# Attention in a transformer layer: sums of exponentials made by accumulating transfers

## The chip, the cores and the metric

The kernel runs on one core of a Trainium2 chip. The core has a matrix engine (PE, with PEld for its weight loads), a vector engine (DVE), an activation engine (ACT), a general engine (POOL) and a queue engine (SP); sixteen DMA engines move data. Each engine works through its own instructions in order and waits on semaphores for the others. The metric is device time in microseconds (us): the median of several executions, lower is better. One execution was also profiled; its views are quoted below with the line numbers of the kernel before.

## The reference

One layer works on 2048 latent tokens of width 1024, with 256 context tokens beside them. It normalises and modulates its input, projects it, mixes tokens by two branches (attention and a gated MLP over chunks), merges them, and ends in a wide MLP. The change touches attention alone, of which the reference says:

```python
def attend(q, k, v):
    s = jnp.einsum('bkgqd,bknd->bkgqn', q, k, preferred_element_type=jnp.float32)
    p = jax.nn.softmax(s, axis=-1).astype(v.dtype)
    return jnp.einsum('bkgqn,bknd->bkgqd', p, v)
...
        k_all = jnp.concatenate([k_c, k_x], axis=2)
        v_all = jnp.concatenate([v_c, v_x], axis=2)
        attn_x = merge_heads(attend_blocked(q_x, k_all, v_all))
```

There are 8 query heads of width 64 on 2 key heads, and 256 + 2048 = 2304 keys. The denominator of the softmax is, for every query and head, the sum of 2304 exponentials. Everything is float32.

## The kernel before

The stages follow one another: projections, attention (about 739 to 1341 us of the profiled span), the merge of the branches, the MLP.

**Units.** Attention is cut into 16 units (class `Unit`), for 4 blocks of 512 queries and 4 pairs of heads, numbered 0 to 15 here. A unit goes over 18 tiles of 128 keys in 9 cycles of two tiles (`PAIR`, `CYCLES`, method `attend`). For a tile, `scores` makes the scores of both heads on PE (line 2488, into a tile s of PSUM), and ACT writes their exponentials (line 2494) to an SBUF tile of 128 partitions (keys) by 2 x 512 columns (heads, queries), 512 KB. The even tile of a cycle is a buffer with the tag p2, the odd one with the tag t4; there are eight of each. The profile leaves numbers out, so they are called p and t there. One cycle later `values` multiplies the exponentials with the values on PE (line 2502, into o), and `gather` adds them into an accumulator.

**Sums.** There are two accumulators a unit. Five of the 18 tiles (2, 5, 8, 11, 14; `ON_VECTOR`) go into one that DVE adds (line 2519); the other thirteen into one that POOL adds, half a tile at a time (line 2522). The first tile of each is taken as it stands, so POOL makes twelve adds of two halves and DVE four. The sums have the tag ac, four buffers. In cycles 2 and 4 of the next unit `join` adds DVE's accumulator into POOL's on DVE, a head at a time (line 2537), and in cycle 5 `sums` multiplies the result with ones on PE (line 2544), which adds over the keys. ACT copies that out (line 2550), and it goes to memory.

**Other work of the stage.** The exponentials are taken against a maximum that must be known before a unit begins. So in every cycle PE also makes plain scores for a later unit (line 2431, into banks m of PSUM, three of them, which line 2544 and others share), and DVE takes their maxima (lines 2436, 2441, into ts). Line 2466 spreads a maximum by eight small transfers a unit. DVE also carries a part of another matrix product (line 428) and, in the last three units, prepares inputs of the merge (lines 1536 and 1543). The last unit has no later unit to make maxima for, and its own division of tiles (`LAST_ON_VECTOR`).

**What sets the order.** Each method issues in the order of the source. A scheduling layer assigns buffers and semaphores; for PE and DVE the order of the attention stage is held as written, for ACT and POOL the scheduler chooses it. A tile's buffer is free once all that read it are done.

Of the kernel before, what the change touches and what calls it, by code (L numbers as in the profile page):

```python
# [14 lines left out]
ALU = mybir.AluOpType  # L15
# [54 lines left out]
PAIR = 2  # L70
CYCLES = NKT // PAIR
AHEAD = 6
ON_VECTOR = (2, 5, 8, 11, 14)
LAST_ON_VECTOR = (2, 4, 7, 8, 9, 12, 13, 14, 15)

OPENING = """
# [24 lines left out]
class Kern:  # L101
# [1308 lines left out]
    def attend(self, units, late, mod, key_loads):  # L1410
        self.psum({"s": 2, "m": 3, "o": 1})
        self.nc.gpsimd.memset(self.rg["q"], 0.0)
        begin = self.here()
        n = len(units)
        pend = []

        def ordered(work):
            at = self.here()
            work()
            self.loads.append(range(at, self.here()))  # L1420

        for i, u in enumerate(units):
            at = lambda k: units[k] if 0 <= k < n else None
            nxt, far, old, older = at(i + 1), at(i + 2), at(i - 1), at(i - 2)
            u.banks()
            for c in range(CYCLES):
                step = nxt if c < AHEAD else far
                if c == 0 and far:
                    far.load()
                if step:  # L1430
                    step.maxima(1)
                group = range(PAIR * c, PAIR * (c + 1))
                for j in group:
                    u.scores(j)
                if step:
                    step.maxima(1)
                owner = u if c else old
                for j in pend:
                    owner.values(j)
                if c == 0:  # L1440
                    if old:
                        old.leave()
                    u.o = self.bank([TB], tag="o")
                if c == 5 and old:
                    old.sums()
                if c == AHEAD and nxt:
                    nxt.reference()
                    ordered(nxt.leading)
                for j in pend:
                    owner.gather(j)  # L1450
                if i and c in (1, 7):
                    next(mod, None)
                if c == 1 and older:
                    older.inverse()
                if c in (2, 4) and old:
                    old.join(c // 4)
                if i == 0:
                    next(key_loads, None)
                if i + c / CYCLES > n - 4 and c % 3 == 1:
                    ordered(lambda: next(late, None))  # L1460
                pend = list(group)
        for _ in mod:
            pass
        owner = units[-1]
        for j in pend:
            owner.values(j)
            owner.gather(j)
        units[-2].inverse()
        total = [self.sb("raw", [TB]) for _ in range(2)]
        for h in range(2):  # L1470
            units[-1].join(h, total)
        self.fixed.append(range(begin, self.here()))
# [924 lines left out]
class Unit:  # L2397
# [109 lines left out]
    def gather(self, j):  # L2507
        k, nc = self.k, self.nc
        pt = self.pts.pop(j)
        e = j in (LAST_ON_VECTOR if self.last else ON_VECTOR)  # L2510
        old = self.acc.get(e)
        if old is None:
            self.acc[e] = pt
            return
        if e not in self.own:
            self.own.add(e)
            self.acc[e] = k.sb("ac", [2, TB])
        if e:
            nc.vector.tensor_tensor(out=self.acc[e], in0=old, in1=pt, op=ALU.add)
        else:  # L2520
            for h in range(2):
                nc.gpsimd.tensor_tensor(  # L2522
                    out=self.acc[e][:, h], in0=old[:, h], in1=pt[:, h], op=ALU.add
                )
# [6 lines left out]
        self.nc.scalar.dma_start(k.at_d[self.b][self.p * P : (self.p + 1) * P, :], oc)  # L2531

    def join(self, h, out=None):
        a, v = self.acc[False], self.acc[True]
        if out is None:
            out = [a[:, i] for i in range(2)]
        self.nc.vector.tensor_tensor(out=out[h], in0=a[:, h], in1=v[:, h], op=ALU.add)
        self.total = out

# [77 lines left out]
```

## Time and profile before

| What | Value |
|---|---|
| Median of 3 runs | 2978.05 us (2977.15 to 2979.62) |
| Profiled execution: time | 2976.75 us |
| Profiled execution: span | 2975.0 us |
| Mean granted clock of PE over the span | 0.993 |
| Busy share: PE, PEld, DVE, ACT, POOL | 97%, 74%, 69%, 47%, 21% |
| POOL's adds of line 2522, 774 to 1345 us | 356 half tiles |
| Instructions | 39180 |

Busy shares are means over stages that differ: POOL works almost only in attention. PE's busy time is modelled from pipelined matmuls, so a busy PE may hide short waits; the length of a unit from the first score matmul to that of the next is firmer. In rows of groups and waits, an arrow names what an engine waited for. In rows of the timeline the first two numbers are start and length in us, and the brackets hold the idle time before.

### The profile page before, as it was taken

How to read it: one execution, taken by the hardware profiler on the slowest of the kernel's cores; microseconds unless marked ns; L12 is line 12 of the kernel's file. 1: busy time of each engine (PE TensorE's matmuls, PEld its weight loads, DVE VectorE, ACT ScalarE, POOL GpSimd, SP SyncE). 2: the span in 40 equal slices, each digit the busy share in tenths (PEclk: the TensorE clock that was granted, in tenths of full speed). 3: DMA queues.
4: the chain of work that ended last, by engine and by line, in shares of the span. 5: the costliest groups of instructions: out<-in, count | busy, mean ns of one | idle time of the engine just before them, and what ended most of it. 6: DMA issues, size and time to landing. Idle time of an engine off the chain costs nothing. (4 is left out here: it accounts for less than half of the span.)

```text
span 2975.0 us, 39180 instructions
## 1 busy us (share of the span) xinstructions
PE 2896.6 (97%) x14126; PEld 2190.4 (74%) x14126; DVE 2056.0 (69%) x3018; ACT 1391.5 (47%) x1993; POOL 633.5 (21%) x444
## 2 busy tenths in 40 slices
PE   8989999989999999999999999999999999999999
PEld 7878788767554554447888878887888888878887
DVE  6866486856888888876555688775766766654555
ACT  6545865552554554553222354444453444444442
POOL 0000000000999999982221100000000000000000
PEclk9999999999999999999999999999999999999999
DMA  8688866876110100117776578888766444457654
GB/s 309 193 296 289 308 203 225 266 243 205 59 37 26 36 30 30 40 47 235 215 211 199 156 249 310 305 288 306 260 217 229 169 140 151 152 174 261 217 213 151
DMA packets 392947, 569.09 MB, mean 191 GB/s; under 512 B 39264, under 2 KB 194576, under 8 KB 392752
## 3 DMA queue, kind: packets, MB, share of 16 engines
q1 hardware_dynamic: 380448, 545.87, 54.6%
q10 hardware_dynamic: 12304, 20.71, 1.9%
q8 instruction: 111, 1.82, 0.3%
q14 instruction: 84, 0.69, 0.1%
HBM read 383.82 MB, written 182.58 MB: 190 GB/s over the span
## 5 line engine op out<-in xcount | busy, mean ns | idle before, releaser
L2441 DVE TENSOR_REDUCE ts<-m 128x1 f32<-128x512 f32 x472 | 300.3, 682 | 55.5 <-PE m L2431 53.4
L2045 DVE TENSOR_TENSOR b<-b,b 128x1024 fp32r<-128x1024 f32 x170 | 200.8, 1222 | 136.1 <-ACT b L2044 135.3
L2522 POOL TENSOR_TENSOR ac<-ac,p 128x512 f32<-128x512 f32 x160 | 266.9, 1691 | 39.5 <-ACT p L2494 39.3
L2044 ACT CAST b<-b 128x1024 fp32r<-128x1024 f32 x170 | 170.6, 1050 | 223.4 <-PE b L1929 100.1
L1928 PE MATMUL b<-b,b 128*128 128x512 f32 x680 | 265.6, 391 | 2.9 <-DVE b L2045 2.9
L1927 PE MATMUL b<-b,b 128*128 128x512 f32 x680 | 266.4, 392 | 1.6 <-DVE f L2066 1.4
L1929 PE MATMUL b<-b,b 128*128 128x512 f32 x680 | 265.1, 390 | 0.0
L2494 ACT ACTIVATE p<-s 128x1024 f32<-128x1024 f32 x149 | 152.2, 1025 | 221.6 <-PE s L2488 203.2
L2522 POOL TENSOR_TENSOR ac<-ac,t 128x512 f32<-128x512 f32 x184 | 251.2, 1393 | 6.3 <-ACT t L2494 6.3
L2488 PE MATMUL s<-h,h 64*128 64x512 f32 x1728 | 227.9, 392 | 0.0
L2488 PEld LDWEIGHTS s<-h,h 64*128 64x128 f32 x1728 | 161.6, 185 | 39.6 <-ACT t L2494 4.1
L1928 PE MATMUL b<-hb,b 128*128 128x512 f32 x446 | 174.3, 391 | 0.0
L1937 DVE TENSOR_TENSOR f<-f,b 128x512 f32<-128x512 f32 x160 | 109.3, 683 | 83.1 <-issue 48.9
L1929 PE MATMUL b<-hb,b 128*128 128x512 f32 x415 | 161.9, 391 | 0.0
L1927 PE MATMUL b<-hb,b 128*128 128x512 f32 x415 | 161.9, 390 | 0.0
L2502 PE MATMUL o<-p,h 128*64 128x512 f32 x596 | 160.1, 619 | 0.0
L1928 PEld LDWEIGHTS b<-b,b 128*128 128x128 f32 x680 | 127.7, 188 | 31.6 <-DVE b L2045 5.0
L1927 PEld LDWEIGHTS b<-b,b 128*128 128x128 f32 x680 | 127.7, 188 | 29.6 <-ACT b L2044 2.3
L1929 PEld LDWEIGHTS b<-b,b 128*128 128x128 f32 x680 | 127.7, 188 | 26.3
L2431 PEld LDWEIGHTS m<-h,h 64*128 64x128 f32 x584 | 60.1, 184 | 117.7 <-DVE ts L2441 94.9
L2502 PE MATMUL o<-t,h 128*64 128x512 f32 x556 | 143.8, 596 | 0.0
L2494 ACT ACTIVATE t<-s 128x1024 f32<-128x1024 f32 x139 | 141.5, 1018 | 0.0
(468 smaller groups left out, 7060.3 us busy)
## 6 DMA issues: line engine op xcount, KB each, us to landing
ao_d<-f SPq DMA_DIRECT2D x224, 256.0 KB
f<-in_w_ff SPq DMA_DIRECT2D x48, 1024.0 KB
b<-ao_d SPq DMA_DIRECT2D x85, 512.0 KB
b<-w2o_d SPq DMA_DIRECT2D x85, 512.0 KB
w2o_d<-f SPq DMA_DIRECT2D x112, 256.0 KB
f<-in_w_in SPq DMA_DIRECT2D x38, 512.0 KB
f<-x_d SPq DMA_DIRECT2D x64, 256.0 KB
hb<-ao_d SPq DMA_DIRECT2D x54, 256.0 KB
```

Source lines behind the costliest of these rows:

```text
L1927: mm(ps, wh, hh, start=start and k == 0, stop=False, skip_group_check=True)
L1928: mm(ps, wh, hl, start=False, stop=False, skip_group_check=True)
L1929: mm(ps, wl, hh, start=False, stop=k == len(w) - 1, skip_group_check=True)
L1937: nc.vector.tensor_tensor(out=out, in0=in0, in1=in1, op=op)
L2044: nc.scalar.copy(h, f32(l))
L2045: nc.vector.tensor_tensor(out=l, in0=f32(l), in1=f32(h), op=ALU.subtract)
L2431: nc.tensor.matmul(out, self.q[0][rows, tok], key[rows], start=True, stop=True)
L2441: nc.vector.tensor_reduce(out=self.mx[:, t, h, c : c + 1], in_=ps[h], axis=AX.X, op=ALU.max)
L2488: nc.tensor.matmul(s[:, h], w[rows], x[rows], start=j < PAIR and n == 0, stop=n == len(terms) - 1, skip_group_check=True,)
L2494: nc.scalar.activation(pt, s, AF.Exp)
L2502: nc.tensor.matmul(self.o[h * HD : (h + 1) * HD, :], k.V[c][:, i, self.kv * HD : (self.kv + 1) * HD], pt[:, h], start=j == 0, stop=j == NK ...
L2522: nc.gpsimd.tensor_tensor(out=self.acc[e][:, h], in0=old[:, h], in1=pt[:, h], op=ALU.add)
```

## The change

Every unit but the last gets three accumulators, and tile j goes to number j modulo 3. Number 0 stays with POOL's adds: tiles 0, 3, 6, 9, 12 and 15, five adds of two halves. Numbers 1 and 2 begin as the exponential tiles 1 and 2 themselves; the tiles that follow (five for each) are added by a transfer that POOL issues, from the tile into the accumulator, with the addition done on the way. `join` becomes two such transfers, of numbers 1 and 2 into number 0, both heads at once. `sums` moves from cycle 5 to cycle 7 of the next unit. The last unit works as before.

```diff
-ON_VECTOR = (2, 5, 8, 11, 14)
+SUMMED = 3
...
-                if c == 5 and old:
+                if c == 7 and old:
                     old.sums()
...
         pt = self.pts.pop(j)
-        e = j in (LAST_ON_VECTOR if self.last else ON_VECTOR)
+        e = j in LAST_ON_VECTOR if self.last else j % SUMMED
         old = self.acc.get(e)
         if old is None:
             self.acc[e] = pt
+            return
+        if e and not self.last:
+            nc.gpsimd.dma_start(out=old, in_=pt, accum_op=ALU.add)
             return
         if e not in self.own:
             self.own.add(e)
...
     def join(self, h, out=None):
-        a, v = self.acc[False], self.acc[True]
+        a, v = self.acc[0], self.acc[1 if self.last else 1 + h]
         if out is None:
-            out = [a[:, i] for i in range(2)]
+            self.nc.gpsimd.dma_start(out=a, in_=v, accum_op=ALU.add)
+            self.total = [a[:, i] for i in range(2)]
+            return
```

The first place is POOL, from the end of unit 1 into unit 2; ac is an accumulator of POOL's, t and p are exponential tiles, and x2 stands for the two halves. Before:

```order
L2522 TENSOR_TENSOR ac_7701<-ac_7701,t_1443_7932 128x512 x2
L2522 TENSOR_TENSOR ac_7701<-ac_7701,p_1448_7962 128x512 x2
L2522 TENSOR_TENSOR ac_7701<-ac_7701,t_1449_7970 128x512 x2
L2522 TENSOR_TENSOR ac_8068<-p_1459_8006,t_1460_8016 128x512 x2
L2522 TENSOR_TENSOR ac_8068<-ac_8068,t_1468_8056 128x512 x2
L2522 TENSOR_TENSOR ac_8068<-ac_8068,p_1476_8088 128x512 x2
```

After the change:

```order
L2525 TENSOR_TENSOR ac_7730<-ac_7730,t_1439_7910 128x512 x2
L2516 DMA t_1389_7642<-p_1446_7946 128x1024
L2516 DMA p_1396_7672<-t_1447_7954 128x1024
L2539 DMA ac_7730<-t_1389_7642 128x1024
L2539 DMA ac_7730<-p_1396_7672 128x1024
L2525 TENSOR_TENSOR ac_8087<-p_1457_7990,t_1466_8038 128x512 x2
L2516 DMA t_1458_8000<-p_1473_8067 128x1024
L2516 DMA p_1465_8030<-t_1474_8075 128x1024
L2525 TENSOR_TENSOR ac_8087<-ac_8087,p_1480_8103 128x512 x2
L2516 DMA t_1458_8000<-t_1481_8111 128x1024
L2516 DMA p_1465_8030<-p_1486_8137 128x1024
```

The adds now alternate with two transfers each, and both joins (line 2539) stand ahead of the next unit's first add.

The second place is DVE in unit 14, around the preparing operations of lines 1536 and 1543; ts takes the maxima of banks m. Before:

```order
L2519 TENSOR_TENSOR ac_12548<-p_2301_12446,t_2313_12499 128x1024
L2441 TENSOR_REDUCE ts_12008<-m_12550 128x1
L2441 TENSOR_REDUCE ts_12008<-m_12551 128x1
L2441 TENSOR_REDUCE ts_12008<-m_12572 128x1
L2441 TENSOR_REDUCE ts_12008<-m_12573 128x1
L2537 TENSOR_TENSOR ac_12085<-ac_12085,ac_12166 128x512
L1536 TENSOR_TENSOR in_12208<-raw_12346,in_12470 128x512
L1543 TENSOR_TENSOR raw_12590<-in_12474,gx_12476 128x512
L2441 TENSOR_REDUCE ts_12008<-m_12597 128x1
L2441 TENSOR_REDUCE ts_12008<-m_12598 128x1
```

After the change:

```order
L2441 TENSOR_REDUCE ts_11893<-m_12420 128x1
L2441 TENSOR_REDUCE ts_11893<-m_12421 128x1
L2441 TENSOR_REDUCE ts_11893<-m_12442 128x1
L2441 TENSOR_REDUCE ts_11893<-m_12443 128x1
L1536 TENSOR_TENSOR in_12086<-raw_12222,in_12341 128x512
L1543 TENSOR_TENSOR raw_12459<-in_12345,gx_12347 128x512
L2441 TENSOR_REDUCE ts_11893<-m_12466 128x1
L2441 TENSOR_REDUCE ts_11893<-m_12467 128x1
```

The add and the join are gone, and the preparing operations stand directly behind the maxima.

## The prediction

> **What bounds the kernel now.** I read the page's engine row first, then the attention stage cut at the first score matmul of each unit of work (windows; columns: length, then busy time and instructions of PE, PEld, DVE, ACT, POOL, granted clock, DMA share, GB/s).
>
> ```profile
> PE 2896.6 (97%) x14126; PEld 2190.4 (74%) x14126; DVE 2056.0 (69%) x3018; ACT 1391.5 (47%) x1993; POOL 633.5 (21%) x444
> ...
> 848.81:885.75 36.94, 36.94 (x233) 18.77 (x230) 32.28 (x46) 18.89 (x21) 35.72 (x25) 1.00 0.11 37
> 885.75:922.73 36.98, 36.98 (x234) 18.79 (x231) 32.33 (x46) 18.89 (x21) 35.75 (x25) 1.00 0.11 36
> 922.73:961.89 39.16, 38.44 (x234) 19.06 (x232) 32.96 (x47) 18.89 (x21) 36.94 (x27) 1.00 0.12 39
> 1110.34:1149.83 39.49, 38.78 (x235) 19.23 (x232) 33.13 (x46) 18.89 (x21) 36.88 (x27) 1.00 0.09 32
> 1186.77:1223.71 36.94, 36.94 (x232) 18.61 (x230) 30.88 (x44) 19.80 (x23) 34.88 (x25) 1.00 0.14 47
> 1223.71:1264.33 40.62, 38.05 (x234) 18.96 (x230) 36.99 (x49) 20.53 (x24) 36.84 (x25) 1.00 0.14 46
> 1264.33:1306.52 42.19, 37.72 (x214) 17.50 (x210) 34.78 (x39) 20.43 (x24) 33.74 (x23) 0.96 0.08 27
> ```
>
> A middle unit takes 36.94 us and PE works through all of it; that is its floor, since the change leaves PE's instructions as they are. POOL is busy 35.7 of the 36.9 but bounds nothing: it lags and catches up. So taking adds from DVE and POOL earns nothing in the middle units. Only where PE waits can time be won, and PE's waits in the whole stage (774 to 1345 us) are these:
>
> ```profile
> PE m L2431 <- DVE ts L2441: 8.5, 6, 3.0
> PE s L2488 <- DMA h<-t: 0.2, 1, 0.2
> ```
>
> PE waits for DVE to empty a bank of m, 8.5 us in six places. Two, 0.7 us each, are in units 5 and 10 (923 and 1110 us: PE is busy that much less than the length); the other four, 7.0 us, fall into units 13 and 14 (1223 to 1306 us), where DVE also prepares the next stage (lines 1536, 1543). DVE ahead of the longest, and then PE's four:
>
> ```profile
> 1285.43 1.67 DVE L2537 TENSOR_TENSOR ac<-ac,ac 128x512 f32<-128x512 f32 x1
> 1287.02 1.77 DVE L1536 TENSOR_TENSOR in<-raw,in 128x512 fp32r<-128x512 f32 x1
> 1288.72 1.74 DVE L1543 TENSOR_TENSOR raw<-in,gx 128x512 f32<-128x512 f32 x1
> 1290.38 1.87 DVE L2441 TENSOR_REDUCE ts<-m 128x1 f32<-128x512 f32 x3
> ...
> 1247.13 0.50 PE L2431 MATMUL m<-h,h 64*128 64x512 f32 x1 [1.34 <-DVE ts L2441]
> ...
> 1261.69 0.50 PE L2431 MATMUL m<-h,h 64*128 64x512 f32 x1 [1.23 <-DVE ts L2441]
> ...
> 1275.86 0.50 PE L2431 MATMUL m<-h,h 64*128 64x512 f32 x1 [1.47 <-DVE ts L2441]
> ...
> 1291.12 0.49 PE L2431 MATMUL m<-h,h 64*128 64x512 f32 x1 [3.00 <-DVE ts L2441]
> ```
>
> A join, then two preparing operations, 5.2 us in a row, stand ahead of the maximum that PE needs at 1291.12. The clock then falls:
>
> ```profile
> 1291.92:1295.33 3.41, 3.41 (x10) 0.97 (x8) 3.41 (x5) 1.03 (x2) 3.15 (x2) 0.50 0.00 0
> ```
>
> **What the change removes.** From DVE: all adds into its accumulator and both joins of every unit but the last. In units 13 and 14 these are
>
> ```profile
> L2519 DVE TENSOR_TENSOR ac<-ac,p 128x1024 f32<-128x1024 f32 x5 | 8.1, 1628 | 3.8 <-ACT p L2494 3.8
> L1536 DVE TENSOR_TENSOR in<-in,in 128x512 fp32r<-128x512 f32 x4 | 6.1, 1517 | 0.0
> L1543 DVE TENSOR_TENSOR raw<-in,gx 128x512 f32<-128x512 f32 x4 | 6.0, 1491 | 0.0
> L2537 DVE TENSOR_TENSOR ac<-ac,ac 128x512 f32<-128x512 f32 x4 | 5.3, 1320 | 0.0
> ...
> L2519 DVE TENSOR_TENSOR ac<-ac,t 128x1024 f32<-128x1024 f32 x2 | 3.5, 1759 | 0.0
> L2519 DVE TENSOR_TENSOR ac<-p,t 128x1024 f32<-128x1024 f32 x2 | 2.8, 1407 | 0.0
> ```
>
> 8.1 + 5.3 + 3.5 + 2.8 = 19.7 us of DVE's 36.99 + 34.78 = 71.8. POOL's adds fall from twelve tiles a unit to five. That shortens DVE's remaining work too, for the two engines hold each other up. A preparing operation takes 1.7 to 1.8 us beside a POOL add and this when POOL is idle:
>
> ```profile
> 1296.66 0.68 DVE L1536 TENSOR_TENSOR in<-raw,in 128x512 fp32r<-128x512 f32 x1
> 1297.26 0.68 DVE L1543 TENSOR_TENSOR raw<-in,gx 128x512 f32<-128x512 f32 x1
> ```
>
> POOL adds will fill about 12.6 of 37 us instead of 35.7, so a third of such operations meet one: 0.68 + 1.1/3, about 1.05 us each. For the 3.00 us wait: less 1.67 for the join and 2 x 0.7 for the shorter pair leaves nothing. The wait of 1.47 has no join ahead but gains the same 1.4; those of 1.34 and 1.23 lose a join or an add of 1.3 to 1.6 us (the means above), and 0.7 or more. I leave 0.5 of the 7.0 us, and 0.7 of the 1.5 us in units 5 and 10: **won 7.3 us** (bounds: 3.0, if only joins directly ahead go, 1.34 + 1.67, to 8.5). The clock at 0.50 for 3.41 us costs half of it, 1.7 us; without the gap before it I count it **won 1.7** (bounds 0 and 1.7). Unit 13 is 40.62 - 36.94 = 3.7 us long over its floor, of which 2.6 are PE's waits; the rest is small slips: **won 0.5** (0 to 1.1). Sum 9.5 us, bounds 3.0 to 11.3.
>
> The Trainium skill ("TensorE: Matmul & The Clock Gate", Part 1) halves the clock after an idle window of about 3.4 us. Here it fell after 3.0, so the trace is stricter. By the page's figure the drop would not hang on this wait and might stay: the time would be 1.7 us higher.
>
> **What it adds.** Per unit twelve accumulating transfers of 512 KB from POOL's queue, ten sums and two joins, in the order shown above: (add, sum into accumulator 1, sum into accumulator 2) five times, join, join. A sum waits on POOL for the previous transfer into its accumulator; the first join for the last sum of accumulator 1, the second for the first. Behind the waiting one stand all of POOL's later adds and sums; ACT waits for those, as an exponential needs a free tile of t4 or p2 (eight each), and PE waits for the exponentials. So the question is whether POOL gets through a unit in 36.94 us. The add, alone on POOL (minimum/median/maximum ns):
>
> ```profile
> L2522 POOL TENSOR_TENSOR ac<-ac,t x172: 1258/1277/2279, 781.9 to 1319.9; 128x512 f32<-128x512 f32 x172
> ```
>
> Two halves, 2.52 us. The trace of before has no transfer from POOL's queue and none that accumulates. The nearest of the same size and row length (4 KB) goes to memory from SP's queue, issued here, with the DMA share of 0.1 us slices from 1428.2 on:
>
> ```profile
> 1428.25 0.33 SPq L1614 DMA_DIRECT2D x_d<-xt  x1
> DMA  0000000059999999899998922896999999974001
> ```
>
> Data run from slice 8 (1429.0) for thirteen slices: 0.75 us after the issue, 1.3 us long. What follows the data shows in a lone 256 KB transfer, issued at 816.61, in slices of 87.5 ns from 816.5:
>
> ```profile
> 816.61 0.35 ACTq L2531 DMA_DIRECT2D at_d<-t  x1
> DMA  0000000000079999996900000000002000000000
> ```
>
> Data end in slice 19, the closing write comes in slice 30, 0.95 us later. An accumulating transfer reads two tiles: its data time is between 1.3 us (second read free) and 2.6 (twice); I take 2.6, because two tiles must be read. The time that an issue holds POOL lies between the 0.33 above and the longest one of the stage:
>
> ```profile
> L2466 SPq DMA_DIRECT2D h<-t x104: 502/587/1652, 803.8 to 1259.2; - x104
> ```
>
> 1.65. I take 1.0, the middle. Landing after the start of the issue: issue + 0.42 + data + 0.95, so 3.0, 5.0 and 5.6 us for low, taken and high. A round is the greater of POOL's work (2.52 + two issues: 3.2, 4.5, 5.8) and two transfers on the engines (2.6, 5.2, 5.2). POOL's unit is four rounds, the last add, two landings (last sum, first join) and an issue:
>
> - low: 4 x 3.2 + 2.52 + 6.0 + 0.3 = 21.6 us
> - taken: 4 x 5.2 + 2.52 + 10.0 + 1.0 = 34.3 us
> - high: 4 x 5.8 + 2.52 + 11.2 + 1.65 = 38.6 us
>
> Two of three are under 36.94, and there the transfers cost PE nothing: PE's own work covers them. They add 12 x 2.6 = 31 us of transfer time a unit to a DMA share of about 0.11, so the engines are nearly full but hold. Without cover each microsecond over is paid in up to 14 units. At 34.3 the joins have landed some 15 us into the next unit; the sums' matmul now stands in its eighth of nine cycles of about 3.9 us, at about 29 us, and doesn't wait. In its old place, the sixth cycle, 21 us, it would have had 6 us less.
>
> The Trainium skill ("Collectives: The Full Stack", Part 3) states that a reducing transfer takes twice a copy's time because it reads two sources. With one read the middle case would be 4 x 4.5 + 2.52 + 7.4 + 1.0 = 28.9 us, also under the floor; no run here shows it yet.
>
> The last unit keeps its adds and joins on POOL and DVE, and the stages behind it are unchanged; they start earlier by what is won.
>
> **Rivals.**
>
> 1. *POOL's queue becomes the bound* (slower). The mechanism is the chain of issues and landings above; it decides once POOL's unit passes 36.94, with doubled data from an issue of about 1.5 us. At 1.65 it is 38.6, 1.7 us over, in some 8 to 14 units after the free tiles are used up: +13 to +23, less the gain: 2982 to 2992. At 2.0 (landing 6.0, round 6.5) it is 26.1 + 2.52 + 12 + 2.0 = 42.6, 5.7 over in about 12 units: +68 - 9 = 3037. With an issue as long as POOL's own add of such a tile, 2.52, it is 48.3, and about 3105. For it: no row shows an issue from POOL, each row has two sources where a copy has one, and at the taken values only 2.6 us are left. Against: half of the bounded range is under the floor, and POOL may lag by several cycles.
> 2. *Too little is won to see.* Lines 1536 and 1543 stay as long as they are (POOL's issues hold DVE as its adds did) and only what joins and adds held up comes back, 3 to 5 us: 2973 to 2975. For it: the pair alone makes the 1.47 us wait. Against: the 0.68 us rows.
> 3. *The sums wait for the joins.* If landings come near 8 us, the joins need some 24 us and in the units after a late start pass 29: PE would stand there 2 to 4 us a unit, 14 times, 2997 to 3025. Against: eight is beyond the high bound.
>
> **How the numbers follow.** The profiled execution took 2976.75 us, its span 2975.0; the median of the runs is 2978.05, 1.3 more. The span falls to 2965.5, the run to 2967.3, and against the median 2978.05 - 9.5 = **2968.5 us**. A change of under 0.2%, 6 us, can't be told from none here. Chances: forecast 0.57, rival 1 0.28, rival 2 0.12, rival 3 0.03. The forecast's own range is 2965 to 2973. With a low end of 2964 about 3 in 100 lie below; of rival 1 the smaller half ends near 3010, so the range is 2964 to 3010 with some 15 in 100 above. Of the forecast's 0.57 some 0.02 win less than 6 us, and rival 2 adds 0.02 above it and 0.10 below. Rival 1 may come out level with its smallest excess (0.01). Faster 0.57, same 0.13, slower 0.30.
>
> **What would show it.** Right: units 13 and 14 near 37 to 38 us, PE's waits on the maxima under 2 us, granted clock 1.00 around 1290 us, POOL's issues near 1 us and no wait of ACT for transfers. Wrong: units of the middle longer than 37 us, ACT waiting for a transfer into t or p, PE after it; or issues of POOL over 1.5 us. If the waits in units 13 and 14 stay with DVE at 1.7 us for the pair, rival 2 it was.

## The result, and the profile after

The changed kernel is slower: a median of 3018.4 us (3017.23 to 3023.74, four runs) against 2978.84 us of the kernel before (2977.15 to 2980.31, four runs), a ratio of 1.0141 with a 95% interval of 1.0129 to 1.0153. The prediction was 2968.5 us, with a range of 2964 to 3010. Times here and below leave out one execution of the run late_dve, which took 3970.53 us at a granted clock of 0.674.

The page of the changed kernel: the busy rows, and the new DMA queue with its packets, MB and share of the sixteen engines over the whole span.

```profile
PE 2904.8 (96%) x14126; PEld 2192.5 (73%) x14126; DVE 1958.2 (65%) x2928; ACT 1392.4 (46%) x1993; POOL 446.9 (15%) x414
...
q0 software_dynamic: 25920, 94.38, 16.7%
```

DVE lost 98 us of work and POOL 187, as the change says, and nothing was won. The windows from unit to unit show where the time went (columns as in the prediction: length, busy time of PE, PEld, DVE, ACT, POOL, granted clock, DMA share, GB/s).

```profile
771.03:814.12 43.09, 38.77 (x233) 19.93 (x230) 24.34 (x39) 18.99 (x21) 26.07 (x25) 0.96 0.94 185
814.12:852.29 38.17, 37.41 (x233) 18.52 (x230) 25.89 (x40) 18.04 (x21) 20.38 (x20) 1.00 0.91 186
929.47:974.72 45.25, 41.52 (x235) 20.76 (x232) 25.13 (x40) 19.34 (x22) 26.88 (x27) 0.92 0.94 184
1209.30:1251.86 42.56, 39.30 (x233) 19.36 (x230) 23.31 (x37) 19.80 (x23) 23.68 (x24) 0.96 0.94 195
1294.04:1344.30 50.26, 42.02 (x212) 19.51 (x213) 30.36 (x30) 20.49 (x25) 28.37 (x28) 0.86 0.94 193
```

From the first unit's start to the last one's it was 567.9 us before and is 608.2 now: the whole loss of 40 us lies there. Over units 1 to 14 the DMA share stands at 0.89 to 0.94 where it was about 0.1. PE's waits from 774 to 1380 us:

```profile
PE s L2488 <- DMA h<-t: 22.5, 13, 4.3
PE m L2431 <- DVE ts L2441: 11.9, 6, 5.7
PE s L2488 <- ACT p L2494: 3.5, 4, 1.7
```

Of these 0.2, 8.5 and nothing were there before. The first row is new. The transfers h<-t are the eight small ones that spread a unit's maximum (line 2466, 0.5 KB each, from SP's queue). Every unit's first score matmuls need them, and in 13 units they wait. SP's queue where it was longest, and PE behind it:

```profile
920.86 8.65 SPq L2466 DMA_DIRECT2D h<-t  x8
...
933.59 0.76 PE L2488 MATMUL s<-h,ones 64*128 64x512 f32 x1 [3.73 <-DMA h<-t]
```

SP's issuing of the eight took 6.5 to 8.65 us here and 4.9 to 6.0 before. The one shown ended as the unit began, at 929.5, and PE waited until 933.6. After three of the longer waits for the row, of 4.32, 3.73 and 2.26 us, the granted clock fell to 0.50 for 3.4 to 6.8 us; after one of 3.13 us, at 1132, it did not. These falls (0.04 of 43 us, 0.08 of 45, 0.04 of 43) cost 7.0 us; 0.14 of 50 us in unit 14, another 7.0, came behind waits for ACT and DVE. Together that is 14 us, against 1.7 before. So 22.3 for the row, 12 for the clock, 3.4 for DVE and 3.5 for ACT make 41 us, about the loss. DVE is no faster beside POOL either, in unit 14:

```profile
1319.56 4.05 DVE L1536 TENSOR_TENSOR in<-raw,in 128x512 fp32r<-128x512 f32 x1
1323.53 3.72 DVE L1543 TENSOR_TENSOR raw<-in,gx 128x512 f32<-128x512 f32 x1
...
1327.91 0.79 PE L2431 MATMUL m<-h,h 64*128 64x512 f32 x1 [5.66 <-DVE ts L2441]
```

The pair of preparing operations takes 7.8 us where it took 3.5, although POOL has far fewer adds.

### The profile page after: what moved, and what is told of

The parts are those of the page before. It is cut to its first block, busy times and chain, and to the rows that moved or that the text cites. A ratio compares the mean times of both kernels' runs of the same rounds, so it can differ in the third digit from the quotient of the medians.

```text
span 3015.4 us, 39121 instructions
## 1 busy us (share of the span) xinstructions
PE 2904.8 (96%) x14126; PEld 2192.5 (73%) x14126; DVE 1958.2 (65%) x2928; ACT 1392.4 (46%) x1993; POOL 446.9 (15%) x414
## 5 line engine op out<-in xcount | busy, mean ns | idle before, releaser
L2488 PE MATMUL s<-h,h 64*128 64x512 f32 x1728 | 238.4, 399 | 1.0 <-ACT p L2494 1.0
L2488 PEld LDWEIGHTS s<-h,h 64*128 64x128 f32 x1728 | 169.3, 188 | 40.4 <-ACT p L2494 3.9
L1927 PEld LDWEIGHTS b<-b,b 128*128 128x128 f32 x680 | 127.7, 188 | 29.5 <-ACT b L2044 2.3
L2431 PE MATMUL m<-h,h 64*128 64x512 f32 (+1 forms) x584 | 125.9, 420 | 12.5 <-DVE ts L2441 12.5
L1940 ACT ACTIVATE f<-f 128x512 f32<-128x512 f32 x96 | 60.5, 630 | 145.5 <-DVE f L1937 145.5
```

The costliest lines, as they stand in the source:

```text
L1927: mm(ps, wh, hh, start=start and k == 0, stop=False, skip_group_check=True)
L1940: nc.scalar.activation(out, src, AF.Relu)
L2431: nc.tensor.matmul(out, self.q[0][rows, tok], key[rows], start=True, stop=True)
L2488: nc.tensor.matmul(s[:, h], w[rows], x[rows], start=j < PAIR and n == 0, stop=n == len(terms) - 1, skip_group_check=True,)
```

## The experiments

Each was timed beside the kernel before on the same chip. The times of before differ a little from chip to chip, so the ratios count.

| Run | Time, us | Ratio to before, 95% interval |
|---|---|---|
| top_early | 3018.75 | 1.0146 (1.0126 to 1.0167) |
| plain_copies | 2960.18 | 0.9948 (0.9932 to 0.9964) |
| half | 3004.01 | 1.0095 (1.0077 to 1.0114) |
| late_dve | 3014.24 | 1.0127 (1.0105 to 1.0149) |
| joins_only | 3029.09 | 1.0187 (1.0170 to 1.0204) |
| joins_pause | 2993.65 | 1.0063 (1.0046 to 1.0080) |
| pool_joins | 3000.36 | 1.0089 (1.0071 to 1.0107) |
| mix | 2982.78 | 1.0028 (1.0016 to 1.0040) |
| mix_early | 2980.01 | 1.0014 (1.0005 to 1.0023) |
| issue_only | 2983.20 | 1.0025 (1.0015 to 1.0034) |
| ten | 2978.19 | 1.0006 (0.9997 to 1.0015) |
| eleven | 2992.97 | 1.0054 (1.0041 to 1.0066) |
| twelve | 3000.12 | 1.0084 (1.0072 to 1.0097) |
| ten_tail | 2984.81 | 1.0029 (1.0018 to 1.0040) |
| ten_tail2 | 2972.88 | 0.9994 (0.9978 to 1.0009) |
| nine_tail | 2966.48 | 0.9968 (0.9959 to 0.9978) |

### Is it the late row?

**top_early**: the changed kernel with the next unit's maximum finished and sent one cycle earlier. The edit adds two lines, so later lines stand two higher.

```diff
-AHEAD = 6
+AHEAD = 5
...
+                if i == 0 and c == 4:
+                    nxt.maxima(2)
```

> Row theory (the eight small transfers of the next unit's maximum row, line 2466, come late through full DMA engines, and PE waits for them and loses its clock): issued one cycle, 3.9 us, earlier they are in time in nearly all units. The waits of line 2488 for h<-t fall from 22.5 us to under 4, the clock loss of 13.7 us by at least 6, and the time from 3018 to 2983-2993 us. Queue theory (POOL's chain of adds and transfers is the bound and the row's wait only stands where another one would come): another wait takes its place, the unit stays near 40 us and the time at or above 3008.

The row's wait went entirely, and the time stayed. Windows of four units:

```profile
777.19:813.96 36.77, 36.77 (x233) 18.43 (x230) 24.36 (x39) 18.90 (x21) 19.95 (x20) 1.00 0.90 180
...
850.75:887.54 36.79, 36.79 (x232) 18.38 (x230) 24.71 (x39) 18.90 (x21) 20.02 (x20) 1.00 0.91 190
...
1049.14:1090.55 41.41, 38.69 (x232) 18.61 (x230) 25.24 (x39) 18.95 (x22) 23.12 (x22) 0.96 0.91 185
1090.55:1130.89 40.34, 37.33 (x233) 18.29 (x230) 26.16 (x40) 19.01 (x22) 23.09 (x22) 1.00 0.92 181
```

ACT's waits of that run, 774 to 1380 us:

```profile
ACT p L2496 <- DMA ac<-p: 50.3, 12, 5.7
ACT t L2496 <- DMA ac<-t: 26.9, 8, 5.0
```

Units 1 to 3 run at the floor, 36.8 us. From unit 4 on they take 39 to 44: ACT now waits for tiles that a join (ac<-p, ac<-t) frees late. So the row theory holds for the first units only, and behind the row lies a second limit at nearly the same height: POOL's transfers run late a little more in each unit, until no free tile is left. POOL issues a unit's first join 7.7 us into the next unit at first, then 13.1, 18.2 and 22.3, and from there on 23 to 27. In the changed kernel the late row slowed PE before that showed: there ACT waited for no sum and no join. POOL's unit is read from its issues into accumulator 2 in the first and the last round of a unit, its two joins, and the first round of the next unit, from unit 8 into unit 9 of the same run:

```profile
1083.89 1.54 POOL L2518 DMA_DIRECT2D p<-t  x1
...
1111.41 0.88 POOL L2518 DMA_DIRECT2D p<-t  x1 [0.92 <-DMA p<-p]
1114.82 0.87 POOL L2541 DMA_DIRECT2D ac<-t  x1 [2.53 <-DMA t<-p]
1120.53 0.86 POOL L2541 DMA_DIRECT2D ac<-p  x1 [4.85 <-DMA ac<-t]
...
1124.14 1.53 POOL L2518 DMA_DIRECT2D p<-t  x1
```

Four rounds take 27.5 us, 6.9 each; then 3.4 to the first join, 5.7 to the second and 3.6 into the next unit: 40.25 us.

### Is it the length of a transfer?

**plain_copies**: the sums copy, they do not add.

```diff
-            nc.gpsimd.dma_start(out=old, in_=pt, accum_op=ALU.add)
+            nc.gpsimd.dma_start(out=old, in_=pt)
...
-        nc.scalar.copy(row, sm)
+        nc.scalar.activation(row, sm, AF.Copy, bias=1.0)
```

> The ten sums of a unit are plain copies of the tile into the accumulator (the additions of twelve tiles out of eighteen are left out, and 1.0 is added to the denominator so that it stays above zero); the two joins still add. The order on every engine, POOL's issues and all waits stay. Row theory by way of full engines: a plain packet of 4 KB takes about half the time, the DMA share falls from 0.91 to about 0.5 and the row's wait from 22.5 us to under 5: 2983-2995 us. If POOL's issues or the mere number of transfers delay the row, the wait stays above 12 us and the time above 3005.

It is 0.5% faster than before, and far below both outcomes of the expectation: not only the row's wait goes. The queue from 774 to 1380 us, first of the changed kernel, then of this one; then its landings and one of its units:

```profile
q0 software_dynamic: 24800, 90.25, 79.6%
...
DMA to landing us min/median/max: 4.6/5.7/8.9
```

```profile
q0 software_dynamic: 24685, 89.85, 44.4%
...
DMA to landing us min/median/max: 2.8/3.4/7.6
...
845.72:882.47 36.75, 36.75 (x233) 18.35 (x230) 25.67 (x39) 18.91 (x21) 19.95 (x23) 1.00 0.62 206
```

Of 606 us, 0.796 spread over 172 transfers (90.25 MB) are 2.8 us of all sixteen engines for an accumulating transfer; for these it is 1.6. A sixth of these are joins, which still add; at 2.8 for each of them the plain ones are left with about 1.3, an estimate. With the engines 0.62 full, the same order of work on every engine runs at the floor, with no wait for the row and none for DVE's maxima. POOL's issues became shorter too (median 0.53 to 0.57 us against 0.87 to 1.2), so this run alone leaves open how much of it is the engines and how much POOL. It does show that the gain that was predicted was there to be had.

**half**: accumulator 2 goes back to DVE's adds, seven transfers a unit.

```diff
-        if e and not self.last:
+        if e == 1 and not self.last:
```

> Only accumulator 1 is summed by transfers, accumulator 2 by DVE as before (line 2519 form), joins by transfers: 7 transfers a unit, not 12. Row theory: the DMA share falls to about 0.55 and the row is rarely late, its wait under 5 us; DVE has its adds back (5 a unit), so its waits in units 13 and 14 stay near 8 to 12 us: 2978-2990 us. Queue theory: POOL's chain has 5 issues less, the same fall; this run tells the size of the cost per transfer, not the two theories apart. If the loss goes with the number of transfers evenly, the time is 2979 + 39 x 7/12 = 3002.

With the accumulating transfers at 0.46 of the engines the row waited 0.2 us, as expected, but the time was 3004, far over the 2978 to 2990 of the expectation, and close to what an even price per transfer gives, for another reason. PE waited 26.8 us for DVE, in 14 places, and DVE's first add of a unit was long:

```profile
L2522 DVE TENSOR_TENSOR ac<-p,t 128x1024 f32<-128x1024 f32 x14 | 54.3, 3875 | 0.0
L2522 DVE TENSOR_TENSOR ac<-ac,t 128x1024 f32<-128x1024 f32 x29 | 36.5, 1259 | 5.4 <-ACT t L2494 5.4
```

3.9 us against 1.26: DVE is held up beside POOL, which is the next question. For the row, this run answers what plain_copies left open: POOL's issues had their full length here (0.88 us in the median), and the row was not late. So it is neither their number nor their length; what the late row goes with is how full the engines are. From 774 us to the last unit's start the DMA share was 0.58 here, 0.61 in plain_copies and 0.92 in the changed kernel, and the row waited 0.2, 0 and 22.5 us; in pool_joins and mix below, with the row in the same place, it waited 13.0 us at 0.80 and 7.8 at 0.68.

### What holds DVE up?

**late_dve**: in units 12 to 14 DVE makes POOL's adds.

```diff
-        if e:
+        if e or (self.b * (NH // 2) + self.p) >= 12:
             nc.vector.tensor_tensor(out=self.acc[e], in0=old, in1=pt, op=ALU.add)
```

> The changed kernel, but in units 12 to 14 DVE makes the sums of accumulator 0 (whole tiles) and POOL only issues transfers. If POOL's pairs of adds hold DVE's preparing operations (lines 1536, 1543): those of units 13 and 14 fall from up to 4.05 us to about 0.7, PE's waits for DVE from 11.9 us to under 5, and with the clock the time falls by 6 to 12 us, to 3006-3012. If POOL's issuing of transfers holds DVE: they stay above 1.5 us, and the time stays at 3014-3022.

Lines 1536 and 1543 fell to 0.67 and 0.69 us and PE's waits for DVE from 11.9 to 2.1 us. So POOL's adds hold DVE, and its issues alone do not. The time did not fall as expected: at 3014.2 us the ratio cannot be told from the changed kernel's 1.0141, for the row (23.7 us) and ACT (9.6) took the room.

**joins_only**: the kernel before with one transfer a unit.

```diff
-                if c in (2, 4) and old:
-                    old.join(c // 4)
+                if c == 2 and old:
+                    old.join(0)
...
-            out = [a[:, i] for i in range(2)]
+            self.nc.gpsimd.dma_start(out=a, in_=v, accum_op=ALU.add)
+            self.total = [a[:, i] for i in range(2)]
+            return
```

The sums move to cycle 7 as in the change.

> The kernel before with one accumulating transfer a unit: the join of DVE's accumulator into POOL's, both heads at once; all sums stay on POOL and DVE as before, and the sums' matmul is two cycles later. If POOL's issuing of transfers changes nothing for DVE: DVE's adds stay at 1.4-1.5 us (whole tiles), DVE loses its joins (1.3 us each), PE's waits for DVE in units 13 and 14 fall from 8.5 to 3-5 us: 2970-2976. If a DVE operation with two SBUF inputs, in a program whose POOL issues transfers, waits until POOL's run of adds ends: DVE's adds rise above 3 us in the mean, PE waits for DVE in most units, and the time is above 2990.

This is the slowest of all, with a DMA queue that is 7% busy. It is the second outcome, though not in every part: DVE's adds of whole tiles took 1.4 to 2.2 us in the mean, not above 3; what grew most is line 428. Its POOL, DVE and PE around one issue:

```profile
1108.00 0.88 POOL L2536 DMA_DIRECT2D ac<-ac  x1 [0.41 <-POOL ac L2522]
1108.61 2.82 POOL L2522 TENSOR_TENSOR ac<-p,t 128x512 f32<-128x512 f32 x2
1111.09 2.82 POOL L2522 TENSOR_TENSOR ac<-ac,t 128x512 f32<-128x512 f32 x2
1113.73 2.60 POOL L2522 TENSOR_TENSOR ac<-ac,p 128x512 f32<-128x512 f32 x2
1124.86 3.51 POOL L2522 TENSOR_TENSOR ac<-ac,p 128x512 f32<-128x512 f32 x2 [8.53 <-ACT p L2494]
...
1110.70 6.18 DVE L428 SCALAR_TENSOR_TENSOR raw<-raw,silu,raw 128x512 f32<-128x512 f32 x1
...
1125.81 1.41 DVE L2519 TENSOR_TENSOR ac<-p,t 128x1024 f32<-128x1024 f32 x1
...
1118.35 0.79 PE L2431 MATMUL m<-h,h 64*128 64x512 f32 x1 [4.97 <-DVE ts L2441]
```

The operation of line 428, alone 0.74 us, lasts until POOL's three adds behind the issue end at 1116.3, and half a microsecond more. After POOL has rested (8.53 us) its adds let DVE in as before: 1.41 us for a whole tile at 1125.81. Over the run, line 428 took 4.95 us in the mean in the six places where POOL ran on from an issue, and 1.83 in the eight where it did not.

**joins_pause**: one more POOL instruction, which makes POOL rest until the transfer has landed.

```diff
             self.nc.gpsimd.dma_start(out=a, in_=v, accum_op=ALU.add)
+            self.nc.gpsimd.tensor_copy(out=v[:, 0, :1], in_=a[:, 0, :1])
```

> The kernel of joins_only (3029 us) with one more POOL instruction behind the transfer of a unit: a copy of one column of the joined accumulator, which waits until the transfer has landed (about 5 us in which POOL rests). Hold theory (POOL's adds directly behind an issue shut out DVE's two-input operations until POOL next rests; joins_only showed L428 at 4.95 us in the mean there and 1.83 elsewhere): the rest ends the hold, L428 falls to 1.9 us or less, PE's waits for DVE from 29.5 us to under 10, and the time to 2972-2990 us, although POOL is now about 36.5 us busy or resting in each unit. Rival (something else of the transfer, its descriptors or its traffic, slows DVE): L428 stays above 3 us and the time at 3020 or above.

Line 428 in the kernel before, in joins_only and in joins_pause (all in the attention stage):

```profile
L428 DVE SCALAR_TENSOR_TENSOR raw<-raw,silu,raw 128x512 f32<-128x512 f32 x14 | 18.4, 1312 | 0.0
```

```profile
L428 DVE SCALAR_TENSOR_TENSOR raw<-raw,silu,raw 128x512 f32<-128x512 f32 x14 | 44.3, 3166 | 0.0
```

```profile
L428 DVE SCALAR_TENSOR_TENSOR raw<-raw,silu,raw 128x512 f32<-128x512 f32 x14 | 21.8, 1560 | 0.0
```

An instruction more, and a stall of POOL, took 35 us off. PE's waits for DVE fell from 29.5 to 3.2 us. The time, 2993.65, is just over the 2972 to 2990 expected: units take 37.5 to 39, since POOL with its twelve adds and the rest is full. The hold theory stands, and the rival, that the transfer itself slows DVE, falls: **adds that follow an issue without a rest shut DVE's two-input operations out until POOL rests.** The Trainium skill ("SBUF — State Buffer", "SBUF: two separate sides") says that the two share a pair of ports, which one instruction locks to its end. The kernel before agrees (a DVE operation waits for one half add: 1.7 against 0.68 us); behind an issue the trace differs, since DVE's wait outlasts several instructions.

### Full engines, or POOL's order?

**pool_joins**: the joins are adds of POOL, ten transfers.

```diff
-            self.nc.gpsimd.dma_start(out=a, in_=v, accum_op=ALU.add)
+            for i in range(2):
+                self.nc.gpsimd.tensor_tensor(out=a[:, i], in0=a[:, i], in1=v[:, i], op=ALU.add)
```

> The two joins of a unit are adds of POOL (two halves each) instead of transfers; the ten sums stay transfers. Chain theory (POOL's order of adds, issues and landings sets the unit: four rounds of 6.9 us, 3.4 for the last sum of accumulator 1, 5.7 for the first join's landing, 3.6 to the next round, 40.25 us in all): the landing of 5.7 and two issues of 0.9 give way to two adds of 2.5, so the unit is about 38 to 39.5 and the time 3000-3012 us. Engine theory (the sixteen DMA engines are full with 12 x 2.8 us and the rest of the traffic): ten transfers fill 28 of 37 us, the DMA share falls to about 0.85, the middle units fall to 37-37.5 us and the time to 2970-2982.

3000.4 is just in the chain theory's interval and far over the engine theory's, but the trace bears out the mechanism of neither: POOL waits for ACT's tiles much of the time, so it had caught up. PE waited 13.0 us for the row and 8.7 for DVE, at a DMA share of 0.80.

**mix** has POOL's joins and gives tiles 16 and 17 to POOL: eight transfers, nine adds of POOL. **mix_early** is the same with the early row.

```diff
+BY_TRANSFER = (0, 1, 2, 0, 1, 2, 0, 1, 2, 0, 1, 2, 0, 1, 2, 0, 0, 0)
...
-        e = j in LAST_ON_VECTOR if self.last else j % SUMMED
+        e = j in LAST_ON_VECTOR if self.last else BY_TRANSFER[j]
```

> Tiles 16 and 17 also go to POOL's own accumulator, and the joins are adds of POOL: eight transfers a unit, nine adds of POOL, none of DVE. Both theories: engines about 0.7 full, POOL about 30 us of 37 busy, so middle units at the floor of 36.75 us that the plain copies showed and the time 2958-2970 us. If DVE's preparing operations (lines 1536, 1543) wait until POOL has run out of adds, PE waits for DVE 5 to 15 us in units 13 and 14 and the time is 2968-2985.

> The mix (eight transfers, 2983 us) with the maximum row one cycle earlier. Row theory: its row waits of 7.8 us and the clock loss behind them go, 2968-2974 us. If the queue or DVE's held operations take over as in the changed kernel with the early row: 2980-2986.

The mix came out at 2982.8, over what both theories gave. That is in the interval of the held DVE, but only in part by its mechanism: line 428 took 2.2 us in the mean and PE waited 5.3 us for DVE, of which 0.9 in units 13 and 14, and 7.8 for the row. With the early row 7.8 became nothing, and DVE's waits rose to 9.2: the second outcome of that expectation.

**issue_only** lets POOL only issue, up to the last unit, and DVE makes one join of unit 14; **ten** does the same in the last unit, where DVE makes all sums; **eleven** and **twelve** differ from ten by the division of tiles. All have the early row. Ten has the table of the mix in units 0 to 11 and goes by j modulo 3 in units 12 to 14, eleven has a 2 for tile 17 in that table, and twelve goes by j modulo 3 throughout; in these three all joins are transfers. The edit of ten, without its table:

```diff
-        if e:
-            nc.vector.tensor_tensor(out=self.acc[e], in0=old, in1=pt, op=ALU.add)
-        else:
-            for h in range(2):
-                nc.gpsimd.tensor_tensor(
-                    out=self.acc[e][:, h], in0=old[:, h], in1=pt[:, h], op=ALU.add
-                )
+        nc.vector.tensor_tensor(out=self.acc[e], in0=old, in1=pt, op=ALU.add)
```

> POOL only issues (except in the last unit): DVE adds accumulator 0, which in units 0 to 11 also has tiles 16 and 17 (seven adds of 1.22 us), in units 12 to 14 five; sums and joins of the other two accumulators stay transfers, ten a unit and twelve in units 12 to 14; the join of unit 14 is DVE's; the maximum row is issued one cycle earlier. Hold theory: DVE's operations stand at their lone lengths (L428 0.74, L1536 and L1543 0.68, adds 1.22). Chain theory: without POOL's adds a round is two issues and the landing, about 6.2 us, so a unit's four rounds and two joins fit 36.8 us: middle units at 36.8-37.5 us, time 2962-2975. If the engines alone are too full (10 x 2.8 + 4 = 32 of 37 us): waits of ACT or PE for transfers of 1-3 us a unit, 2975-3000.

> As issue_only, but POOL adds nothing anywhere: DVE also makes all sums of the last unit, and all joins are transfers (ten transfers a unit, twelve in units 12 to 14). Hold theory: with no add of POOL nothing holds DVE; the 14.6 us join and the waits of 8.7 us in the last unit go, middle units stay at 37.8 us (DVE has 7 adds): 2970-2978 us. Otherwise as issue_only, 2980-2985.

> As ten, but tile 17 goes to accumulator 2: six adds of DVE and eleven transfers in units 0 to 11, 11 x 2.8 + 4 = 35 us of the engines' time in a unit of 37. If DVE's load sets the 37.8 us of issue_only: middle units 37.0-37.4 us, 2962-2972. If the engines are too full at eleven, ACT or PE waits for transfers and it is slower than ten.

> The changed kernel's division of tiles (five adds for accumulator 0, twelve transfers) with the early row, but all of POOL's adds are DVE's. Engine theory for the changed kernel's unit of 40 us (twelve transfers of 2.8 us and 4 us of others do not fit 36.8): the unit cannot be under 37.6 us, lag builds up as with the early row alone, ACT waits for transfers in the later units, 2980-3010. Chain theory (POOL's adds between the issues lengthened the rounds to 6.9 us): without them a round is about 6 us and the middle units are 36.8-37.4 us, 2958-2970.

In issue_only DVE's operations had their lone lengths, as expected (line 428 0.74, adds 1.22), but middle units took 37.8 us, because DVE with seven adds is 32 of 37 us busy and PE waits for it half a microsecond here and there; and in the last unit POOL's adds held a join for 14.6 us. Ten, without that, came to 2978, level with before and at the upper end of its expectation. Middle and late units of ten, eleven and twelve:

```profile
852.99:890.84 37.85, 37.32 (x234) 18.62 (x231) 32.18 (x47) 18.91 (x21) 8.76 (x10) 1.00 0.87 177
...
1043.39:1081.23 37.84, 37.31 (x232) 18.63 (x230) 32.17 (x47) 18.90 (x21) 8.75 (x10) 1.00 0.86 176
```

```profile
846.62:883.41 36.79, 36.79 (x232) 18.37 (x230) 31.05 (x46) 18.91 (x21) 9.33 (x11) 1.00 0.93 193
...
1071.71:1111.78 40.07, 37.05 (x234) 18.80 (x232) 31.75 (x47) 19.32 (x22) 9.66 (x11) 1.00 0.86 176
```

```profile
845.31:882.10 36.79, 36.79 (x232) 18.37 (x230) 30.00 (x45) 18.91 (x21) 9.31 (x11) 1.00 0.94 193
...
1035.44:1075.01 39.57, 37.29 (x233) 18.18 (x230) 29.99 (x45) 18.92 (x22) 10.50 (x12) 1.00 0.95 193
```

Ten holds its pace; eleven and twelve start at the floor and fall to 39 to 40 us once the free tiles are gone. Twelve has no add of POOL and still does 39.6 at a share of 0.95, so the chain theory, which gave 36.8 to 37.4 without these adds, falls. The transfers alone keep a unit over the floor, in two parts. The engines are busy for 0.95 x 39.6 = 37.6 us, 0.8 over the floor. The other 2 us they stand idle, and that is mostly one place, between the two joins of a unit, where POOL waits for the first to land before it issues the second (twelve):

```profile
1058.77 0.88 POOL L2535 DMA_DIRECT2D ac<-t  x1 [1.91 <-DVE rg_q L2450]
1064.92 0.87 POOL L2535 DMA_DIRECT2D ac<-p  x1 [5.28 <-DMA ac<-t]
```

From 1064.0 to 1066.5 us the DMA share is 0.14. So the full engines and the wait in POOL's order each have a part in the 2.8 us over the floor, and the wait costs time because engines this full have nothing to spare. POOL's adds cost the rest: top_early has the same transfers with them and is some 19 us slower than twelve. What is not settled is eleven, whose late units run at a share of only 0.86 to 0.87: there POOL waits up to 7.5 us for one landing while others could be issued, and how that divides with full engines the runs do not say.

### Both costs avoided

In **ten_tail** tile 17 is added to accumulator 2 by POOL, behind the wait for that accumulator's last transfer, so after a rest; **ten_tail2** does this with tile 16 into accumulator 1 as well; **nine_tail** makes also the second join an add, behind the landing of the first. DVE makes the adds of accumulator 0. The early row stays, and tile 16 belongs to accumulator 0 in ten_tail, to accumulator 1 in the other two. The place of ten_tail2:

```diff
         if e and not self.last:
-            nc.gpsimd.dma_start(out=old, in_=pt, accum_op=ALU.add)
+            if j in (16, 17):
+                for h in range(2):
+                    nc.gpsimd.tensor_tensor(out=old[:, h], in0=old[:, h], in1=pt[:, h], op=ALU.add)
+            else:
+                nc.gpsimd.dma_start(out=old, in_=pt, accum_op=ALU.add)
             return
```

> As ten, but tile 17 of every unit but the last goes to accumulator 2 by a POOL add, which stands behind the wait for that accumulator's last transfer: ten transfers, six adds of DVE, one of POOL a unit, also in units 12 to 14. Hold theory (only adds directly behind an issue hold DVE, those behind a rest do not) and engine theory (ten transfers fit): middle units 36.8 us as the first ones of eleven, without its lag, 2962-2970 us. If POOL's add holds DVE all the same: DVE operations above 2 us and 2972-2985.

> As ten_tail, but tile 16 goes to accumulator 1 by a POOL add too: ten transfers, five adds of DVE, two of POOL. The same units of 36.8 us and less of DVE in units 12 to 14: 2958-2968 us. If two adds of POOL at the unit's end make its queue late: waits of ACT for transfers, 2970-2985.

> As ten_tail2, but the second join is a POOL add behind the landing of the first: nine transfers, five adds of DVE, three of POOL. Engines about 0.8 full. 2958-2966 us if the engines' share still costs something at ten; equal to ten_tail2 within 3 us if not; and 2970-2985 if that add, which stands ahead of the next unit's issues, makes them late or holds DVE.

ten_tail missed: most of its units are 36.8 us up to unit 8, then ACT waits for joins 36 us in all, as in eleven (51). ten_tail2 cannot be told from before, and so missed its 2958 to 2968 too. nine_tail is faster, at 2966.5 us, 0.9968 (0.9959 to 0.9978) of before, half a microsecond over its expectation. One of its middle units, the two largest of PE's waits, 774 to 1400 us, and line 428:

```profile
886.62:924.20 37.58, 37.58 (x233) 18.81 (x231) 31.64 (x45) 18.90 (x21) 16.16 (x16) 1.00 0.79 162
...
PE s L2490 <- ACT p L2496: 3.5, 1, 3.5
PE s L2490 <- DMA h<-t: 1.3, 2, 1.1
...
L428 DVE SCALAR_TENSOR_TENSOR raw<-raw,silu,raw 128x512 f32<-128x512 f32 x14 | 10.9, 776 | 0.0
```

With the engines at 0.79 and POOL's adds behind rests, line 428 is near its lone length. Units 13 and 14, where the gain was predicted, take 37.6 and 35.6 us against 40.6 and 42.2, 9.7 us less; unit 12 takes 5.2 more by the wait of 3.5 us for ACT and the clock behind it. So the predicted gain (9.5 us) is there where it was predicted, in a kernel that keeps three quarters of the change's transfers. That the whole run wins about as much is in part luck: from the first unit's start to the last one's it is only 3.1 us shorter than before, and the rest lies outside.

## Why the prediction was wrong

**The bound and the gain** were right. PE's floor is near 37 us (36.75 in the runs without waits), and the waits for DVE in units 13 and 14 are worth what was priced: 9.5 us predicted, 9.7 won there in nine_tail, where DVE still adds but is seldom held. Over the whole run nine_tail won 10 us and plain_copies 15, with other changes in them.

**The pieces of a transfer** were nearly right: data 2.6 us taken and 2.8 measured, issue 1.0 and 0.86 to 1.25, landing 5.0 and 5.7 in the median, though 6.8 for those from a t into a p, and up to 8.9. The Trainium skill's two sources of a reducing transfer ("Collectives: The Full Stack", Part 3) agree with 2.8 us against the estimated 1.3 of a plain one.

**The step that failed** is "the engines are nearly full but hold", and with it "there the transfers cost PE nothing". It took the 31 us of transfers as throughput alone. With 12 x 2.8 = 33.6 us and some 4 us of other traffic (a share of 0.11 of 37) the unit has 37.6 us of transfers: over the floor. Twelve shows that this does not hold, at 0.95. And before lag shows, whatever small transfer needs the engines comes late. The working asked what POOL's queue waits for, and never what SP's queue has to send through the same engines: the row, 22.5 us of PE's waits, and 7 us of clock behind them. Its wait stands in the prediction's own list with 0.2 us, and got no term.

**The round** was the mis-sized term in POOL's unit. It was set to the greater of POOL's work and two data times, 5.2 us; it measured 6.9, because the sums of a round share the engines and the next round waits for a landing on top. The unit so became 40.25 us, not 34.3. That is rival 1, which had 0.28 and prices of 2982 to 3037 for 38.6 to 42.6 us; its lag and its waits of ACT are what top_early shows. Its condition, an issue of about 1.5 us or more, was not met (0.86 to 1.25), and in the changed kernel itself the loss came by the row before the lag could: that 3018 lies between its prices is partly luck. The range was cut at its smaller half, 3010, and that was too low.

**Lines 1536 and 1543** were the second wrong term: 1.05 us each, from the share of time that POOL adds fill. They measured 1.0 to 2.9 in the mean and up to 4.05, and PE's waits for DVE rose from 8.5 to 11.9 us instead of falling to 1.2. The share of time was the wrong measure: an add behind an issue does not share. Rival 2 put the hold on POOL's issues; late_dve and issue_only show that it is the adds behind them.

**The sums in the eighth cycle** do not wait in the changed kernel, as said; in top_early, eleven and twelve they do (6 to 7 us in each). (A cycle is 36.94 / 9 = 4.1 us, not 3.9; the 29 us are right.)

## What to carry to other kernels

Before work is moved to transfers, add up the engines' time of everything in the stage, and then ask which small transfer on another queue the critical engine waits for: it comes late well before the sum reaches one (here 7.8 us of waits at 0.68, 22.5 at 0.92). A limit that free buffers hide at first shows only after several units, so look at the late ones, and after removing a wait look for what stands at the same height. On an engine that issues transfers itself, keep adds off the place directly behind an issue, or let it rest in between.

## What the runs showed of the hardware

- An accumulating transfer of 512 KB between SBUF tiles took 2.8 us of all sixteen engines, landed 5.7 us after its issue in the median and held POOL for 0.86 to 1.25 us (1.6 right behind another issue). The plain copy took about 1.3, an estimate, landed after 3.4 and held POOL for 0.53 to 0.57.
- Behind an issue POOL's adds, as long as they follow each other without a rest, kept DVE's two-input operations out: 6.2 us for one of 0.74 us in joins_only, 17.1 us for a whole-tile add of 1.22 us in the last unit of mix_early. The maxima, which read one tile, were not held (0.68 us before and in joins_only). The same adds after a rest cost DVE about one half add. Why the hold lasts past an instruction no run tells.
- Eight transfers of 0.5 KB from SP's queue took 4.9 to 6.0 us to issue at a DMA share near 0.1, and 6.5 to 8.65 us at 0.92.
